# Where ScalarE's first "up" conversion stands in the experts' loop, and which engine makes the gate rows of the first layer

## Chip, cores and metric

The kernel runs on one core of one Trainium2 chip. The metric is the device time of one execution in microseconds (us). A profiled execution also leaves its span (first to last instruction) and, for each instruction, its start, its duration and what it waited for.

## The reference

The reference is two layers of a diffusion backbone over 512 latent and 256 context tokens of width 1024. Each layer has a token mixer (retention and pooling) and then a hierarchical mixture of 32 SwiGLU experts. Only the second half matters here:

```
h  = modulate(x, norm2_g, sh2, sc2)            # latent tokens, and in layer 0 the context tokens too
y  = sum over the token's 2 experts of  w * ((silu(h @ w_gate[e]) * (h @ w_up[e])) @ w_down[e])
x  = x + g2 * y        # latent rows use g2, context rows use cg2
```

`w_gate` and `w_up` of an expert are 1024 x 512, `w_down` is 512 x 1024, all float32: 2 MB each, 6 MB an expert, 32 experts a layer. The first layer routes 768 tokens (latent and context), the second only the 512 latent ones. So in the first layer a row that comes out of an expert is multiplied by `g2` or by `cg2`, as its token is latent or context; in the second layer all rows use `g2`.

## The kernel before

**Slots.** Each expert works on 96 slots (`CAP`). For each expert GpSimd gathers the slots' rows of `h` by an indirect DMA (`fetch`, L1215), TensorE turns them (`turn`, L1227), and VectorE and ScalarE copy the result out of PSUM (`turned`, L1231: `xh` on VectorE at L1234, `xl` on ScalarE at L1235).

**Weights.** All weights stream from HBM as 1 MB halves into a pool of 7 buffers named `raw`, issued by SyncE in one fixed order: for each expert two halves of gate, two of down (of the expert before) and two of up. `pump` (L141) issues the next transfers when VectorE's low conversion has been queued. ScalarE makes the float16 high part (`hi_`, which calls `conv_hi`, L1337), VectorE the float16 rest (`lo_`, which calls `conv_lo`, L1342). The second half of down is used as it is (`native`). TensorE multiplies high and low parts in three passes (`mm3`, L418 to L420), and the native half in float32 (L1285).

**The loop.** `for e in range(1, NE)` (L1545) writes out by hand the order of work of one expert on every engine; each engine runs its own instructions in that order. TensorE's order in a turn of the loop is: gate product of expert e+1, down product of e in two halves (n = 0 and 1), the transposes for e+2, up product of e+1. ScalarE's order is: the two gate conversions of e+2, `act_gate`, the first down conversion of e+1, `down_out` of half 0, the first up conversion of e+2 (L1575), `down_out` of half 1, the copy `xl`, the second up conversion. `down_out` (L1289) moves a half of the down product out of PSUM, times the routing weight of the slot.

**The gate rows.** `rows_of(e)` (L1487) gives the 96 x 1024 rows of gate factors of the expert's slots. In the second layer (`nv == 1`) these are the plain `g2` rows. In the first (`nv == 2`) `gate_rows` (L1291) works them out on GpSimd in two operations (L1296, L1297), from a tile `g2r` that holds `g2` and the difference of `cg2` and `g2`, and a flag of each slot (`ctx`, 1 for a context token). GpSimd then multiplies the expert's rows by them (`scatter`, L1305), starts the scatter that adds the rows to the stream in HBM (L1309), and the next `fetch`. Two `ye` tiles hold the experts' rows in turn; the gate rows lie in the second half of the same tile.

**The last expert** leaves the loop early: it skips scatter, and `last_down` (L1439) and `add_last` (L1451) add it on chip to the rows that were loaded back from HBM.

Of the kernel before, what the change touches and what calls it, by code (L numbers as in the profile page):

```python
# [14 lines left out]
ALU = mybir.AluOpType  # L15
# [11 lines left out]
CAP = 96  # L27
# [14 lines left out]
def kernel(ctx: ExitStack, tc: tile.TileContext, a: dict, out: bass.AP):  # L42
# [10 lines left out]
    def G(shape, dt, name):  # L53
        return pg.tile(shape, dt, name=name, tag="G")
# [4 lines left out]
    def W(shape, dt, name="wt"):  # L59
        return pw.tile(shape, dt, name=name, tag="W")  # L60
# [4 lines left out]
    def P(shape, name="pt"):  # L65
        return pp.tile(shape, F32, name=name, tag="P")

    V, A, Q, T = nc.vector, nc.scalar, nc.gpsimd, nc.tensor
# [317 lines left out]
    def mod_rows(l, sec, nv=2, tmp_=True):  # L386
        t = (R if tmp_ else G)([128, nv, D], F32, "modrow")
        nc.scalar.dma_start(out=t, in_=modr[l][sec, 0:nv].unsqueeze(0).to_broadcast([128, nv, D]))
        return t
# [791 lines left out]
    def make_sel(dst, posb, tiles, eng=None):  # L1181

        for i in tiles:
            (eng or Q).tensor_scalar(dst[:, i, :], iot1, posb[:, i, :], None, op0=ALU.is_equal)
# [28 lines left out]
    def fetch(l, xg, si):  # L1213

        Q.indirect_dma_start(  # L1215
            out=xg, out_offset=None, in_=hs[l],
            in_offset=bass.IndirectOffsetOnAxis(ap=si, axis=0), bounds_check=(6 - 2 * l) * 128 - 1,
            oob_is_err=False)

    def turn(xg):  # L1220

        out = []
        for r in range(2):
            pt = pp.tile([128, KC, CAP], F16, name="pgx", tag="P")
            for c in range(KC):
                o = r * D + c * 128
                T.transpose(pt[:, c, :], xg[0:CAP, o:o + 128], ident16[0:CAP, 0:CAP])  # L1227
            out.append(pt)
        return out

    def turned(pts):  # L1231
        xh = W([128, KC, CAP], F16, "xh")
        xl = W([128, KC, CAP], F16, "xl")
        V.tensor_copy(xh, pts[0])  # L1234
        A.copy(xl, pts[1])  # L1235
        return xh, xl
# [16 lines left out]
    def gate_up(w, xe, out_ps):  # L1253
        hi, lo = w
        xh, xl = xe
        for f in range(4):
            sl = slice(f * 128, (f + 1) * 128)
            for c in range(KC):
                mm3(out_ps[:, f, :], hi[:, c, sl], lo[:, c, sl], xh[:, c, :], xl[:, c, :], c == 0, c == KC - 1)

    def act_gate(pg_):
        sg = W([128, 4, CAP], F32, "sg")
        A.activation(sg, pg_, AF.Silu, scale=IWS)
        return sg

    def act_mult(pu, sg):

        V.scalar_tensor_tensor(sg[:, 0:2], pu[:, 0:2], IWS, sg[:, 0:2], op0=ALU.mult, op1=ALU.mult)
        V.tensor_tensor(sg[:, 2:4], pu[:, 2:4], sg[:, 2:4], op=ALU.mult)

    def act_split(sg):
        at = W([128, 2, 2, CAP], F16, "at")
        A.copy(at[:, 0], sg[:, 0:2])  # L1273
        V.tensor_tensor(at[:, 1], sg[:, 0:2], at[:, 0], op=ALU.subtract)
        return at

    def down_mm(w, raw, at, sg, n):

        hi, lo = w
        sl = slice(n * 512, (n + 1) * 512)  # L1280
        pt = P([128, 512], "pdn")
        for f in range(2):
            mm3(pt[0:CAP, :], at[:, 0, f, :], at[:, 1, f, :], hi[:, f, sl], lo[:, f, sl], f == 0, False)
        for f in range(2, 4):
            T.matmul(pt[0:CAP, :], lhsT=sg[:, f, :], rhs=raw[:, f - 2, sl], start=False, stop=(f == 3))  # L1285
        return pt

    def down_out(pt, wcol, yt, n):
        A.activation(yt[0:CAP, n * 512:(n + 1) * 512], pt[0:CAP, :], AF.Copy, scale=wcol)  # L1289

    def gate_rows(yg, ctx, g2r, nv):  # L1291

        if nv == 1:
            return [g2r[0:CAP, 0, n * 512:(n + 1) * 512] for n in range(2)]
        gn = yg[0:CAP, 1, :]
        Q.tensor_scalar(gn, g2r[0:CAP, 1, :], ctx, None, op0=ALU.mult)  # L1296
        Q.tensor_tensor(gn, gn, g2r[0:CAP, 0, :], op=ALU.add)  # L1297
        return [gn[:, n * 512:(n + 1) * 512] for n in range(2)]

    def scatter(l, yg, si, gs, eng):  # L1300

        yt = yg[:, 0, :]
        for n in range(2):
            yn = yt[0:CAP, n * 512:(n + 1) * 512]
            eng.tensor_tensor(yn, yn, gs[n], op=ALU.mult)  # L1305
        scatter_rows(l, yg, si)
# [9 lines left out]
    def new_conv(l, e, m):  # L1316
        if m == 2:
            t = G([128, 2, 2, 1024], F16, "wd")
            convs[l, e, m] = (t[:, 0], t[:, 1])
            return  # L1320
        convs[l, e, m] = (G([128, KC, 512], F16, "whi"), G([128, KC, 512], F16, "wlo"))
# [10 lines left out]
    def conv_hi(l, e, m, hf):  # L1332
        k_ = 4 if m < 2 else 2
        sl = slice(k_ * hf, k_ * hf + k_)
        hi, lo = convs[l, e, m]
        t = get("exp", l, e, m, hf)
        A.activation(hi[:, sl, :], t, AF.Copy, scale=WS)  # L1337
        return lo[:, sl, :], t, hi[:, sl, :]

    def conv_lo(low):  # L1340
        lo, t, hi = low
        V.scalar_tensor_tensor(lo, t, WS, hi, op0=ALU.mult, op1=ALU.subtract)  # L1342
        pump()

    def moe(l, h2, rt, pe0, nt, post_load=None):
# [80 lines left out]
        def load_latent(eng=nc.sync):  # L1426
            for i in range(4):
                eng.dma_start(out=xl[i // 2][:, i % 2, :], in_=xs[l][i * 128:(i + 1) * 128, :])

        def sel_transposed(pe):  # L1430

            pt = P([128, 512], "pst")
            for i in range(4):
                T.matmul(pt[0:CAP, i * 128:(i + 1) * 128], lhsT=pe[:, i, :], rhs=ident16, start=True, stop=True)
            t = W([128, 512], F16, "selT")
            A.copy(t[0:CAP], pt[0:CAP])
            return t
# [28 lines left out]
        def hi_(e, m, hf):  # L1466
            if hf == 0:
                new_conv(l, e, m)
            lows.append(conv_hi(l, e, m, hf))

        def lo_():
            conv_lo(lows.pop(0))

        def native(e):
            natives[l, e] = get("exp", l, e, 2, 1)

        def weight(e):
            return rt.sv[0:CAP, 0, e:e + 1]

        def slot(e):  # L1480
            return rt.si[:, e:e + 1]
# [5 lines left out]
        def rows_of(e):  # L1487
            yg = yes[e % 2]
            return yg, gate_rows(yg, rt.sv[0:CAP, 1, e:e + 1], g2r, nv)
# [12 lines left out]
        g2r = mod_rows(l, 3, nv, False)  # L1502
# [42 lines left out]
        for e in range(1, NE):  # L1545

            nx, nx2 = e + 1 < NE, e + 2 < NE
            act_mult(put, sg)
            at = act_split(sg)
            if lows:  # L1550
                lo_()
            sgd = sg
            w, raw = convs.pop((l, e, 2)), natives.pop((l, e))
            yg, gs = rows_of(e)
            if e == NE - 2:
                st["depth"] = NR - 2
            if e == NE - 4:
                pes = W([128, nt, CAP], F16, "pe")
                make_sel(pes, posm[:, :, NE - 1:NE], range(4))
            if not nx:  # L1560
                break
            pgt = P([128, 4, CAP], "pgate")
            gate_up(convs.pop((l, e + 1, 0)), xe, pgt)
            if nx2:
                for hf in range(2):
                    hi_(e + 2, 0, hf)
                    lo_()
            sg = act_gate(pgt)
            hi_(e + 1, 2, 0)
            native(e + 1)  # L1570
            lo_()
            pt = down_mm(w, raw, at, sgd, 0)
            down_out(pt, weight(e), yg[:, 0, :], 0)
            if nx2:
                hi_(e + 2, 1, 0)  # L1575
            pt = down_mm(w, raw, at, sgd, 1)
            down_out(pt, weight(e), yg[:, 0, :], 1)
            scatter(l, yg, slot(e), gs, Q)
            if nx2:
                xn = turned(turn(xg[:, e % 2]))  # L1580
                lo_()
                hi_(e + 2, 1, 1)
                if e + 4 < NE:
                    fetch(l, xg[:, e % 2], slot(e + 4))
            else:
                xl += [G([128, 2, D], F32, "xl") for _ in range(2)]
                load_latent()
                selT = sel_transposed(pes)
                if post_load:
                    post_load()  # L1590
            put = P([128, 4, CAP], "pup")
            gate_up(convs.pop((l, e + 1, 1)), xe, put)
            xe = xn
            if e == 8:
                rt.overflow()
# [205 lines left out]
```

## Time and profile before

| what | value |
|---|---|
| median of 3 runs | 1801.63 us (1801.56 to 1804.43) |
| time of the profiled execution | 1806.32 us |
| its span | 1804.5 us |
| TensorE busy | 1607.9 us, 89% of the span |
| VectorE busy | 1360.3 us, 75% |
| ScalarE busy | 1019.1 us, 56% |
| GpSimd busy | 1040.6 us, 58% |
| DMA moved | 542.33 MB, 301 GB/s over the span |
| granted TensorE clock, mean | 0.943 of full speed |

The shares are means over stages of different kinds. The experts' loops run from about 388 to 970 us (first layer) and from about 1240 to 1787 us (second layer). The two loops are the same code over weights of the same size, except for the gate rows and the number of routed rows, so each can be read against the other.

### The profile page before, as it was taken

How to read it: one execution, taken by the hardware profiler on the slowest of the kernel's cores; microseconds unless marked ns; L12 is line 12 of the kernel's file. 1: busy time of each engine (PE TensorE's matmuls, PEld its weight loads, DVE VectorE, ACT ScalarE, POOL GpSimd, SP SyncE). 2: the span in 40 equal slices, each digit the busy share in tenths (PEclk: the TensorE clock that was granted, in tenths of full speed). 3: DMA queues.
4: the chain of work that ended last, by engine and by line, in shares of the span. 5: the costliest groups of instructions: out<-in, count | busy, mean ns of one | idle time of the engine just before them, and what ended most of it. 6: DMA issues, size and time to landing. Idle time of an engine off the chain costs nothing. (4 is left out here: it accounts for less than half of the span.)

```text
span 1804.5 us, 43422 instructions
## 1 busy us (share of the span) xinstructions
PE 1607.9 (89%) x19059; PEld 1175.6 (65%) x19059; DVE 1360.3 (75%) x1454; ACT 1019.1 (56%) x1040; POOL 1040.6 (58%) x530
## 2 busy tenths in 40 slices
PE   6999998869897898988888999987999898999986
PEld 3577775556765676766664667645777777777763
DVE  5665567788788999887777786777977777778774
ACT  4433342337666667666664544434867667777762
POOL 1222224546898899999986232253455556666653
PEclk9999999969998999899998999987999999999998
DMA  9644455459998999999997165657999999999993
GB/s 386 246 143 182 149 204 216 149 197 326 381 367 337 355 391 393 382 369 378 364 370 241 55 216 170 238 198 247 371 391 373 377 393 388 399 398 391 395 373 124
DMA packets 127294, 542.33 MB, mean 301 GB/s; under 512 B 21595, under 2 KB 22667, under 8 KB 91001
## 3 DMA queue, kind: packets, MB, share of 16 engines
q1 hardware_dynamic: 105384, 507.87, 73.2%
q0 software_dynamic: 18000, 20.56, 4.8%
q10 hardware_dynamic: 3712, 11.04, 1.6%
q8 instruction: 153, 2.51, 0.6%
q14 instruction: 45, 0.36, 0.1%
HBM read 538.72 MB, written 45.69 MB: 324 GB/s over the span
## 5 line engine op out<-in xcount | busy, mean ns | idle before, releaser
L1342 DVE SCALAR_TENSOR_TENSOR wlo<-raw,whi 128x2048 f16<-128x2048 f32 x248 | 609.9, 2493 | 158.7 <-ACT whi L1337 157.5
L1337 ACT ACTIVATE whi<-raw 128x2048 f16<-128x2048 f32 x248 | 472.4, 1910 | 264.4 <-DMA raw<-in_exp_w_up_dram 212.5
L420 PEld LDWEIGHTS <-wlo 128*128 128x128 f16 x4512 | 454.8, 101 | 129.2 <-issue 97.9
L418 PEld LDWEIGHTS <-whi 128*128 128x128 f16 x4512 | 455.6, 101 | 45.6 <-issue 16.3
L419 PEld LDWEIGHTS <-whi 128*128 128x128 f16 x4512 | 455.2, 101 | 44.3 <-issue 15.0
L419 PE MATMUL pgate<-xl,whi 128*128 128x96 f16 x2048 | 299.2, 217 | 88.9 <-ACT xl L1235 88.6
L418 PE MATMUL pgate<-xh,whi 128*128 128x96 f16 x2048 | 302.7, 217 | 7.7 <-DVE xh L1234 5.5
L420 PE MATMUL pgate<-xh,wlo 128*128 128x96 f16 x2048 | 299.3, 217 | 0.0
L1305 POOL TENSOR_TENSOR ye<-ye,modrow 96x512 f32<-96x512 f32 x62 | 160.9, 2595 | 212.0 <-ACT ye L1289 212.0
L418 PE MATMUL pup<-xh,whi 128*128 128x96 f16 x2048 | 266.3, 206 | 0.0
L420 PE MATMUL pup<-xh,wlo 128*128 128x96 f16 x2048 | 266.0, 206 | 0.0
L419 PE MATMUL pup<-xl,whi 128*128 128x96 f16 x2048 | 266.0, 206 | 0.0
L1285 PE MATMUL pdn<-raw,sg 128*96 128x512 f32 x512 | 247.2, 606 | 0.0
L1309 POOL DMA_INDIRECT xs<-ye,si x63 | 192.3, 3052 | 23.6 <-POOL ye L1305 17.7
L1342 DVE SCALAR_TENSOR_TENSOR wd<-raw,wd 128x2048 f16<-128x2048 f32 x64 | 161.7, 2526 | 12.3 <-ACT wd L1337 11.9
L1305 POOL TENSOR_TENSOR ye<-ye 96x512 f32<-96x512 f32 x62 | 133.8, 2171 | 41.8 <-ACT ye L1289 40.0
L1296 POOL TENSOR_SCALAR ye<-modrow,sv 96x1024 f32<-96x1024 f32 x32 | 148.0, 4626 | 1.3
L1285 PEld LDWEIGHTS pdn<-raw,sg 128*96 128x96 f32 x512 | 85.6, 167 | 90.7 <-issue 72.1
L1337 ACT ACTIVATE wd<-raw 128x2048 f16<-128x2048 f32 x64 | 122.1, 1908 | 13.3 <-DMA raw<-in_exp_w_down_dram 13.2
L418 PE MATMUL pdn<-wd,at 128*96 128x512 f16 x256 | 99.8, 390 | 17.7 <-ACT at L1273 10.2
L405 DVE SCALAR_TENSOR_TENSOR wlo<-raw,whi 128x2048 f16<-128x2048 f32 (+1 forms) x36 | 84.8, 2361 | 39.4 <-ACT whi L404 39.4
L1215 POOL DMA_INDIRECT xg<-hs,si x62 | 89.2, 1439 | 34.3 <-issue 15.6
(310 smaller groups left out, 3123.9 us busy)
## 6 DMA issues: line engine op xcount, KB each, us to landing
raw<-in_exp_w_gate_dram SPq DMA_DIRECT2D x128, 1024.0 KB
raw<-in_exp_w_up_dram SPq DMA_DIRECT2D x128, 1024.0 KB
raw<-in_exp_w_down_dram SPq DMA_DIRECT2D x128, 1024.0 KB
raw<-in_ada_w_dram SPq DMA_DIRECT2D x32, 1024.0 KB
raw<-in_w_in_dram SPq DMA_DIRECT2D x20, 1024.0 KB
raw<-in_ada_dram SPq DMA_DIRECT2D x16, 1024.0 KB
raw<-in_w_out_dram SPq DMA_DIRECT2D x8, 1024.0 KB
xs<-xr ACTq DMA_DIRECT2D x10, 512.0 KB
```

What stands on the lines that cost most here:

```text
L405: V.scalar_tensor_tensor(lo, t, WS, hi, op0=ALU.mult, op1=ALU.subtract)
L418: T.matmul(o, lhsT=lh, rhs=rh, start=first, stop=False)
L419: T.matmul(o, lhsT=lh, rhs=rl, start=False, stop=False)
L420: T.matmul(o, lhsT=ll, rhs=rh, start=False, stop=last)
L1215: Q.indirect_dma_start(out=xg, out_offset=None, in_=hs[l], in_offset=bass.IndirectOffsetOnAxis(ap=si, axis=0), bounds_check=(6 - 2 * l) * ...
L1285: T.matmul(pt[0:CAP, :], lhsT=sg[:, f, :], rhs=raw[:, f - 2, sl], start=False, stop=(f == 3))
L1296: Q.tensor_scalar(gn, g2r[0:CAP, 1, :], ctx, None, op0=ALU.mult)
L1305: eng.tensor_tensor(yn, yn, gs[n], op=ALU.mult)
L1309: Q.indirect_dma_start(out=xs[l], out_offset=bass.IndirectOffsetOnAxis(ap=si, axis=0), in_=yg[0:si.shape[0], 0, :], in_offset=None, bounds ...
L1337: A.activation(hi[:, sl, :], t, AF.Copy, scale=WS)
L1342: V.scalar_tensor_tensor(lo, t, WS, hi, op0=ALU.mult, op1=ALU.subtract)
```

## The change

Two edits. In the first layer the row of `g2` of the slots is made by one VectorE operation in place of two GpSimd ones. In the loop the first up conversion on ScalarE stands after the second `down_out` and the copy `xl`, no longer between the two `down_out`.

```diff
         gn = yg[0:CAP, 1, :]
-        Q.tensor_scalar(gn, g2r[0:CAP, 1, :], ctx, None, op0=ALU.mult)
-        Q.tensor_tensor(gn, gn, g2r[0:CAP, 0, :], op=ALU.add)
+        V.scalar_tensor_tensor(gn, g2r[0:CAP, 1, :], ctx, g2r[0:CAP, 0, :], op0=ALU.mult, op1=ALU.add)
         return [gn[:, n * 512:(n + 1) * 512] for n in range(2)]
...
             pt = down_mm(w, raw, at, sgd, 0)
             down_out(pt, weight(e), yg[:, 0, :], 0)
-            if nx2:
-                hi_(e + 2, 1, 0)
             pt = down_mm(w, raw, at, sgd, 1)
             down_out(pt, weight(e), yg[:, 0, :], 1)
             scatter(l, yg, slot(e), gs, Q)
             if nx2:
                 xn = turned(turn(xg[:, e % 2]))
+                hi_(e + 2, 1, 0)
                 lo_()
                 hi_(e + 2, 1, 1)
```

`Q` is GpSimd, `V` VectorE. `hi_(e + 2, 1, 0)` is the conversion of the first half of `w_up` of expert e+2. On VectorE the new operation stands where `rows_of(e)` is called (L1554): after `act_split` and the low conversion of the second up half, ahead of the low conversions of gate.

## Rows read from the trace of the kernel before

**Rows 1.** Timeline of GpSimd: scatter starts of experts 0, 2, 30, in both layers.
```profile
411.25 1.64 POOL L1309 DMA_INDIRECT xs<-ye,si  x1 [0.28 <-POOL ye L1305]
...
457.65 3.65 POOL L1309 DMA_INDIRECT xs<-ye,si  x1 [0.28 <-POOL ye L1305]
...
958.38 1.60 POOL L1309 DMA_INDIRECT xs<-ye,si  x1 [0.49 <-POOL ye L1305]
...
1261.85 1.62 POOL L1309 DMA_INDIRECT xs<-ye,si  x1 [0.29 <-POOL ye L1305]
...
1304.02 3.64 POOL L1309 DMA_INDIRECT xs<-ye,si  x1 [0.28 <-POOL ye L1305]
...
1773.38 1.57 POOL L1309 DMA_INDIRECT xs<-ye,si  x1 [0.28 <-POOL ye L1305]
```
**Rows 2.** Windows: busy us by engine, then granted clock, DMA share, GB/s.
```profile
458.00:940.00 482.00, 422.05 (x6020) 327.63 (x6017) 413.99 (x258) 315.68 (x265) 445.05 (x163) 0.95 0.98 370
580.00:660.00 80.00, 73.29 (x1120) 58.60 (x1119) 78.96 (x44) 52.85 (x47) 68.23 (x26) 0.96 0.97 368
1304.00:1757.00 453.00, 415.38 (x6127) 324.88 (x6125) 340.81 (x256) 317.23 (x266) 270.58 (x110) 0.97 1.01 389
1760.00:1763.00 3.00, 3.00 (x42) 3.00 (x40) 2.52 (x5) 1.16 (x2) 2.72 (x2) 0.52 0.28 116
```
**Rows 3.** DMA queues, 458 to 940 us: packets, MB, share of 16 engines.
```profile
q1 hardware_dynamic: 29937, 167.67, 88.9%
q0 software_dynamic: 7619, 10.02, 8.6%
```
**Rows 4.** DMA queues, 1304 to 1757 us.
```profile
q1 hardware_dynamic: 30136, 168.50, 93.5%
q0 software_dynamic: 7632, 6.87, 6.4%
```
**Rows 5.** DMA queues, 1440 to 1720 us.
```profile
q1 hardware_dynamic: 18895, 105.90, 95.0%
q0 software_dynamic: 4906, 3.74, 5.7%
```
**Rows 6.** GpSimd by line, 458 to 940 us: busy, mean ns, idle before.
```profile
L1296 POOL TENSOR_SCALAR ye<-modrow,sv 96x1024 f32<-96x1024 f32 x27 | 127.8, 4732 | 1.1
L1305 POOL TENSOR_TENSOR ye<-ye 96x512 f32<-96x512 f32 x52 | 113.6, 2198 | 18.2 <-ACT ye L1289 16.6
...
L1297 POOL TENSOR_TENSOR ye<-ye,modrow 96x1024 f32<-96x1024 f32 x27 | 75.7, 2803 | 2.3
```
**Rows 7.** VectorE by line, 458 to 940 us.
```profile
L1342 DVE SCALAR_TENSOR_TENSOR wlo<-raw,whi 128x2048 f16<-128x2048 f32 x107 | 288.6, 2734 | 50.7 <-ACT whi L1337 50.7
```
**Rows 8.** VectorE by line, 1304 to 1757 us.
```profile
L1342 DVE SCALAR_TENSOR_TENSOR wlo<-raw,whi 128x2048 f16<-128x2048 f32 x107 | 241.1, 2287 | 81.8 <-ACT whi L1337 81.7
```
**Rows 9.** Source line L328, whole span: ns min/median/max, first and last start.
```profile
L328 DVE SCALAR_TENSOR_TENSOR acc<-raw,sel,acc x56: 1273/1279/2222, 107.4 to 1157.0; 128x1024 f32<-128x1024 f32 x56
```
**Rows 10.** Waits, 1304 to 1757 us: total us, times, longest us.
```profile
PE pgate L419 <- ACT xl L1235: 37.6, 21, 3.8
```
**Rows 11.** Timeline near the end of layer two's loop: TensorE, ScalarE, VectorE.
```profile
1752.82 0.25 PE L1227 MATMUL pgx<-ident,xg 96*128 96x96 f16 x2
...
1755.93 1.91 ACT L1337 ACTIVATE whi<-raw 128x2048 f16<-128x2048 f32 x1 [3.37 <-DMA raw<-in_exp_w_up_dram]
1757.75 0.67 ACT L1289 ACTIVATE ye<-pdn,sv 96x512 f32<-96x512 f32 x1
1758.32 0.78 ACT L1235 COPY xl<-pgx 128x768 f16<-128x768 f16 x1
...
1759.15 0.20 PE L419 MATMUL pgate<-xl,whi 128*128 128x96 f16 x1 [1.96 <-ACT xl L1235]
...
1761.46 2.28 DVE L1342 SCALAR_TENSOR_TENSOR wlo<-raw,whi 128x2048 f16<-128x2048 f32 x1
...
1771.04 0.21 PE L418 MATMUL pup<-xh,whi 128*128 128x96 f16 x1
```

## The prediction

> **What bounds the kernel now.** I read the page first, then the experts' loop of each layer as a window, since only these stages change, and then queues, lines and waits inside them. GpSimd's scatter starts give the pace of an expert: from expert 2 to 30 the first layer takes 958.38 - 457.65 = 500.7 us, 17.88 us an expert, and the second 1773.38 - 1304.02 = 469.4 us, 16.76 us [rows 1]. The code and the weights are the same size, so 1.12 us an expert is what the first layer pays for gate rows and for more routed rows. The windows show 27 experts each (482 / 17.88 and 453 / 16.76).
>
> In the second layer the transfers set the pace: the DMA engines' share is 1.01, at 389 GB/s, and no compute engine is near its limit but TensorE, 415 of 453 us busy [rows 2]. By queue, weights (q1) and gathers and scatters (q0) take 93.5 + 6.4 = 99.9% [rows 4]; its quiet middle has 95.0 + 5.7 = 100.7% [rows 5]. The reader should see that more speed of an engine cannot shorten that middle. In the first layer the queues take 88.9 + 8.6 = 97.5% [rows 3]. Scatters weigh more there, and that stays; but 2 to 3% of the time the transfers are not all asked for. Two engines are the suspects. GpSimd is busy 445 of 482 us, VectorE 414 of 482, and 78.96 of 80 us in the stretch 580 to 660 [rows 2]. VectorE's low conversion frees the buffer for the next transfer, and it takes 2734 ns against 2287 ns in the second layer [rows 7, 8].
>
> A second loss is the order on ScalarE. The first up conversion waits for its transfer, and behind it, in order, stand `down_out` and the copy `xl`, for which TensorE waits before the next gate product: 37.6 us in 21 waits in the second layer [rows 10]. While transfers set the pace this wait costs nothing by itself; after the last transfer it does.
>
> **The change, part by part. Gate rows.** GpSimd loses (127.8 + 75.7) / 27 = 7.5 us an expert [rows 6] of 445 / 27 = 16.5 us [rows 2], and is left with 9.0 us, far from the pace. VectorE gains one operation of 96 x 1024 float32 with a scalar per partition. Nearest row: the same kind at 128 x 1024 takes 1279 ns by the median, 1273 to 2222 [rows 9]. I take 1.28 us; the upper end is 2.22 us. VectorE now has 414 / 27 = 15.3 us an expert against 340.8 / 27 = 12.6 in the second layer [rows 2]. The loop of the second layer has all of GpSimd's remaining work, so I take its 12.6 and add 1.28: 13.9 us. If no conversion gets faster it is 15.3 + 2.2 = 17.5, still under 17.88 but no longer in the stretch 580 to 660. The operation writes the half of `ye` that the multiplies of two experts ago read; these ended about an expert's time earlier, so no wait. Behind it on VectorE stand the two gate conversions, and behind those the issue of two transfers, which go out 1.28 us later with three or more 1 MB transfers still in the queue: hidden while that queue is filled, 1.28 x 27 = 35 us at most if it were not.
>
> *What it gives in the first layer's loop.* Lower bound 0, if the missing 2.5% is the scatters' own irregularity. If the queues reach the second layer's share, 482 x (1 - 97.5 / 99.9) = 11.6 us [rows 3, 4]; if they reach the share of its quiet middle, 482 x (1 - 97.5 / 100.7) = 15.3 us [rows 5]. I take 11.6, the row of the same loop with its same interruptions. At the loop's start, experts 0 to 2, the first layer takes 457.65 - 411.25 = 46.4 us and the second 42.2 [rows 1]: 0 to 4.2 us, I take 2.
>
> The low conversions are longer by 2734 - 2287 = 447 ns beside GpSimd's gate rows [rows 7, 8]. The Trainium skill ("SBUF — State Buffer", Who interferes with whom) says that a VectorE instruction with two SBUF inputs and a GpSimd instruction that reads SBUF exclude each other for the whole instruction. By that rule the new operation could itself stand behind a whole GpSimd multiply of 2.2 us (an estimate by that page and the multiply's row), which would put VectorE at about 12.6 + 1.28 + 2.2 = 16.1 us; still under the pace, so the sum stays. The trace agrees in kind: conversions are slowed, though not each by a whole GpSimd operation.
>
> **Order on ScalarE.** Nothing is added or removed; the conversion issues no transfer itself, and on ScalarE it is moved past a `down_out` of 0.67 us and a copy of 0.78. On the queue of VectorE its low conversion keeps its place. In the last expert but one of layer two, the transposes end at 1753.07, so both could end by about 1754.5, while the weights came at 1755.93 [rows 11]: 1.4 us of margin, so the conversion is not later. TensorE no longer waits. If the transposes ended after the weights' arrival, the conversion would be late by the difference, hidden by the queued transfers. So in the paced part of layer two I take 1 us, of 0 to 453 x (1 - 99.9 / 100.7) = 3.6 us that its queues leave unused [rows 4, 5].
>
> *At the ends.* After the last up weights, TensorE's work is what is left. In layer two it waits 1.96 us for `xl` until 1759.15, and its granted clock over the next 3 us is 0.52 [rows 2, 11], nearly the 1.2 GHz level of its two (1.2 and 2.4 GHz), after that idle: 3 x 0.48, about 1.5 us more. So at least 3.5 us. TensorE's lead may also build up, by 37.6 / 27 = 1.4 us an expert, until the next thing it needs, the low part of the second up half: that ends at 1761.46 + 2.28 = 1763.7, and the up product starts at 1771.04 [rows 11]. So at most 7.3 us; I take 5, half-way. The first layer's end has the same code, then the overflow check and conversions for the next layer, which may swallow it: 0 to 7.3, I take 3.
>
> **Sum.** 11.6 + 2 + 1 + 5 + 3 = 22.6 us. The profiled execution takes 1806.3 us, 1.8 over its span; 1806.3 - 22.6 = 1783.7. It lies 4.7 us over the median of the runs, so against 1801.6 the forecast is 1779.0. A difference under 0.2%, 3.6 us, is about what cannot be told from none.
>
> **Rivals.**
> *Transfers at their limit already.* The first layer's loop keeps its 500 us since its scatters (8.6% against 6.4% of the engines [rows 3, 4]) use what seems unused; only ends gain. For it: a share of 0.98 in the window [rows 2]. Against: 370 GB/s there, 389 in the second loop. Time: 1801.6 - 5 - 2 = 1794.6. A page speaks for it: the Trainium skill ("SBUF — State Buffer", A bandwidth-pool intuition that's wrong) gives about 358 GB/s from HBM to a core, by which both loops are above the limit and nothing is left to gain. The trace differs, with 389 GB/s over 453 us [rows 2].
> *VectorE becomes the bound.* Conversions stay at 2734 ns because the multiplies, not the gate rows, slow them, and the new operation takes 2.2 us. Place: 580 to 660, where VectorE is 99% busy; 4.5 experts x 2.2 = 10 us there, and no lead for TensorE in layer one. Time: 1801.6 + 10 - 5 = 1806.6, slower. It decides if VectorE's time an expert passes the transfers' pace. Against: 12.6 us in layer two beside the same multiplies.
> *The change does nothing.* TensorE's wait for `xl` is replaced by one for weights just as late, also at the ends, and GpSimd's work was off the path: 1801.
>
> **How the numbers follow.** Forecast 0.66, transfers at their limit 0.20, nothing 0.08, VectorE the bound 0.06. All lower terms together give 3.5 us, all upper ones 15.3 + 4.2 + 3.6 + 7.3 + 7.3 = 37.7 us, hence 1764 to 1798; leaving out the corners and the two last rivals, the range is 1767 to 1797. Faster 0.86, same 0.08, slower 0.06.
>
> **What would show it.** In the profile after: GpSimd's lines of gate rows gone and 32 VectorE operations of about 1.3 us; low conversions of the first layer near 2.29 us; an expert of the first layer near 17.4 us and one of the second near 16.7; queue shares in the first loop near 100%; no wait of the gate product for `xl`; the up product of the last expert of layer two nearer to its low conversion. The prediction is wrong if the queue shares stay at 97.5% while VectorE and GpSimd have fallen, if VectorE's new operation takes over 2 us, or if ScalarE stands idle before the moved conversion with its weights already there.

## The result, and the profile after

The changed kernel takes 1779.6 us by the median (1778.7 to 1781.3 in 4 runs) against 1801.6 us, in the ratio 0.988 with an interval of 0.986 to 0.990: about 22 us faster, at 1.2% some six times what can be told from no change. Run again beside another 13 runs of the kernel before it gave 0.989 (0.986 to 0.992). The forecast was 1779.0 us. The total came out; half of the terms did not, and most of what follows is about them. The profiled execution took 1778.7 us, 0.9 under its own median, where that of before lay 4.7 over its own; so the two traces differ by 27.6 us, and some 5.6 of these are not the change's. To keep them out I took a second profile of the kernel before (label `e13_before_again`, 1796.0 us), and below a difference is shown against both.

Windows of the profile after, 27 experts of each layer as in [rows 2], then the two stretches in which experts 8 to 12 of the first layer and the former bottleneck lie. Columns: busy us of TensorE, weight load, VectorE, ScalarE, GpSimd, then granted clock, DMA share, GB/s.

```profile
444.00:926.00 482.00, 422.95 (x6169) 320.88 (x6168) 381.20 (x292) 326.43 (x272) 242.43 (x112) 0.98 1.00 379
1277.00:1730.00 453.00, 413.20 (x6098) 315.01 (x6096) 341.18 (x258) 323.14 (x269) 216.02 (x110) 0.98 1.01 389
533.14:600.89 67.75, 61.52 (x915) 47.18 (x916) 61.56 (x61) 47.90 (x41) 45.05 (x16) 0.97 0.99 380
580.00:660.00 80.00, 76.22 (x1159) 58.82 (x1157) 70.11 (x50) 57.86 (x49) 48.54 (x22) 1.00 1.02 402
```

GpSimd has 242 / 27 = 9.0 us an expert instead of 16.5, VectorE 381 / 27 = 14.1 instead of 15.3, with an operation more. In 580 to 660, where it was 79 of 80 us busy [rows 2], VectorE now has 10 us free. The second layer's row moves little. The granted clock of the first loop is 0.98 and was 0.95 [rows 2]; TensorE has some 60 us of the 482 idle in both, and no run separates the clock from the rest. The queues of the first window, to be read beside [rows 3]:

```profile
q1 hardware_dynamic: 31220, 171.21, 90.3%
q0 software_dynamic: 7858, 10.47, 9.0%
```

Together 99.3% and not 97.5%. VectorE by line in the same window, beside [rows 7] (busy us, mean ns, idle before):

```profile
L1341 DVE SCALAR_TENSOR_TENSOR wlo<-raw,whi 128x2048 f16<-128x2048 f32 x109 | 252.3, 2330 | 69.2 <-ACT whi L1336 69.2
L1296 DVE SCALAR_TENSOR_TENSOR ye<-modrow,sv 96x1024 f32<-96x1024 f32 x28 | 35.7, 1274 | 0.0
L1274 DVE TENSOR_TENSOR at<-sg,at 128x192 f16<-128x192 f32 x27 | 9.9, 367 | 7.0 <-ACT at L1273 7.0
...
L1268 DVE SCALAR_TENSOR_TENSOR sg<-pup,sg 128x192 f32<-128x192 f32 x27 | 9.4, 348 | 0.0
```

The low conversion fell from 2734 to 2330 ns, and the gate row costs 1274 ns. A row that I had not read ahead of the prediction fell further: the small subtraction that makes the low part of `at` took 1004 ns in the first trace of before, and takes 367. GpSimd by line shows what is left there, beside [rows 6]:

```profile
L1304 POOL TENSOR_TENSOR ye<-ye 96x512 f32<-96x512 f32 x54 | 115.2, 2150 | 217.0 <-ACT ye L1289 216.9
```

Waits of TensorE in the same window (total us, times, longest us). The wait for `xl` [rows 10] is gone, here and in the second layer. Another has taken its place: the down product waits for the cast `at`, which stands on ScalarE behind the second up conversion.

```profile
PE pdn L418 <- ACT at L1273: 38.1, 24, 4.1
...
PE pgate L418 <- DVE xh L1234: 20.7, 17, 2.8
```

The scatter starts of experts 2 and 30, the anchors of [rows 1], in both layers:

```profile
444.13 3.37 POOL L1308 DMA_INDIRECT xs<-ye,si  x1 [0.28 <-POOL ye L1304]
...
932.42 1.55 POOL L1308 DMA_INDIRECT xs<-ye,si  x1 [0.28 <-POOL ye L1304]
...
1275.13 3.36 POOL L1308 DMA_INDIRECT xs<-ye,si  x1 [0.28 <-POOL ye L1304]
...
1744.69 1.55 POOL L1308 DMA_INDIRECT xs<-ye,si  x1 [0.28 <-POOL ye L1304]
```

An expert of the first layer takes (932.42 - 444.13) / 28 = 17.44 us (17.88 before), one of the second 16.77 (16.76). These anchors mislead a little, since the second `down_out` no longer stands behind a conversion and so the scatter itself comes earlier. From here on an expert is timed by VectorE's first multiply of the up product (line 1268). The table has the us between these multiplies, one profile a row.

| kernel | L1 0→2 | 2→8 | 8→12 | 12→31 | L2 2→30 | 30→31 |
|---|---|---|---|---|---|---|
| before, first profile | 54.9 | 106.0 | 78.9 | 333.6 | 472.8 | 15.2 |
| before, second profile | 55.1 | 104.1 | 77.3 | 332.0 | 473.8 | 13.6 |
| order only (e1) | 55.6 | 106.9 | 70.5 | 339.6 | 473.0 | 11.4 |
| gate row only (e2) | 48.9 | 106.5 | 70.0 | 332.7 | 474.4 | 13.6 |
| order, gate row for 0 to 2 (e11) | 48.1 | 107.8 | 77.4 | 345.0 | 472.8 | 11.4 |
| order, gate row for 7 to 14 (e12) | 54.9 | 107.9 | 66.6 | 339.4 | 472.9 | 11.4 |
| after plus a VectorE operation (e9) | 50.5 | 105.7 | 72.6 | 337.4 | 473.0 | 11.4 |
| after | 46.9 | 107.0 | 67.8 | 333.5 | 472.6 | 11.4 |
| after, again (e6) | 47.8 | 106.7 | 68.0 | 331.8 | 473.3 | 11.4 |

Between before and after the reader should see three places and nothing else: the start of the first loop, 55 to 47 us; experts 8 to 12 of it, 77 to 79 down to 68; and the last step of the second loop, 13.6 or 15.2 to 11.4. The paced parts (2→8, 12→31, 2→30) do not move between before and after. Each row is one execution: those of e1, e11 and e12 stood 8 us under, 10 over and 7 over the median of their kernels; so the columns say where, and the medians how much.

In e1, e11 and e12, which have the new order and gate rows on GpSimd for most experts, 12→31 is long. So the loss behind expert 8 is not tied to the column 8→12. Two other sums show it in every row. The step 8→9 takes 23.8 to 26.2 us in the four profiles with the gate row of expert 9 on GpSimd (before twice, e1, e11), and 20.8 to 21.9 in the other five (in the second loop, without gate rows, 20.7 to 22.3). And 8→31 takes 412.5 and 409.3 us in before, 410.1 with the order alone, 422.5 in e11, against 401.2 and 399.9 after.

### The profile page after: what moved, and what is told of

Its sections match the earlier page's. It is cut to its first block, busy times and chain, and to the rows that moved or that the text cites. A ratio compares the mean times of both kernels' runs of the same rounds, so it can differ in the third digit from the quotient of the medians.

```text
span 1776.9 us, 43385 instructions
## 1 busy us (share of the span) xinstructions
PE 1591.1 (90%) x19059; PEld 1146.2 (65%) x19059; DVE 1315.5 (74%) x1486; ACT 1028.0 (58%) x1040; POOL 752.6 (42%) x466
## 5 line engine op out<-in xcount | busy, mean ns | idle before, releaser
L1341 DVE SCALAR_TENSOR_TENSOR wlo<-raw,whi 128x2048 f16<-128x2048 f32 x248 | 568.8, 2315 | 158.9 <-ACT whi L1336 158.6
L419 PEld LDWEIGHTS <-whi 128*128 128x128 f16 x4512 | 442.8, 98 | 71.1 <-issue 41.8
L418 PEld LDWEIGHTS <-whi 128*128 128x128 f16 x4512 | 443.3, 98 | 45.6 <-issue 16.3
L420 PEld LDWEIGHTS <-wlo 128*128 128x128 f16 x4512 | 442.7, 98 | 36.2 <-issue 5.0
L418 PE MATMUL pgate<-xh,whi 128*128 128x96 f16 x2048 | 269.8, 207 | 31.6 <-DVE xh L1234 31.0
L419 PE MATMUL pgate<-xl,whi 128*128 128x96 f16 x2048 | 269.7, 207 | 0.4 <-ACT xl L1210 0.2
L420 PE MATMUL pgate<-xh,wlo 128*128 128x96 f16 x2048 | 269.7, 207 | 0.0
L1304 POOL TENSOR_TENSOR ye<-ye,modrow 96x512 f32<-96x512 f32 x62 | 124.2, 2018 | 260.0 <-ACT ye L1289 260.0
L1336 ACT ACTIVATE wd<-raw 128x2048 f16<-128x2048 f32 x64 | 122.2, 1910 | 78.9 <-DMA raw<-in_exp_w_down_dram 78.9
L1308 POOL DMA_INDIRECT xs<-ye,si x63 | 135.6, 2152 | 21.3 <-POOL ye L1304 17.7
L1215 POOL DMA_INDIRECT xg<-hs,si x62 | 121.7, 1962 | 32.2 <-issue 24.2
L418 PEld LDWEIGHTS <-at 128*96 128x96 f16 x256 | 32.4, 127 | 113.0 <-ACT at L1273 78.4
```

The source lines that it names most:

```text
L418: T.matmul(o, lhsT=lh, rhs=rh, start=first, stop=False)
L419: T.matmul(o, lhsT=lh, rhs=rl, start=False, stop=False)
L420: T.matmul(o, lhsT=ll, rhs=rh, start=False, stop=last)
L1215: Q.indirect_dma_start(out=xg, out_offset=None, in_=hs[l], in_offset=bass.IndirectOffsetOnAxis(ap=si, axis=0), bounds_check=(6 - 2 * l) * ...
L1308: Q.indirect_dma_start(out=xs[l], out_offset=bass.IndirectOffsetOnAxis(ap=si, axis=0), in_=yg[0:si.shape[0], 0, :], in_offset=None, bounds ...
```

## Experiments

My theory after the result: gate rows on GpSimd cost time only through VectorE, whose operations they slow, in two places where VectorE has no slack; the transfers set the rest. Rivals: GpSimd's own time was the bound (late scatters and gathers); the gain is spread over all experts; the order on ScalarE gives the larger part.

**Each part alone.** `e1_order_only` puts the gate row of the changed kernel back on GpSimd:

```
-        V.scalar_tensor_tensor(gn, g2r[0:CAP, 1, :], ctx, g2r[0:CAP, 0, :], op0=ALU.mult, op1=ALU.add)
+        Q.tensor_scalar(gn, g2r[0:CAP, 1, :], ctx, None, op0=ALU.mult)
+        Q.tensor_tensor(gn, gn, g2r[0:CAP, 0, :], op=ALU.add)
```

> The moved conversion alone; the gate rows stay on GpSimd in two operations. The prediction's terms for the order are 1 us in the paced part of layer two and 5 + 3 us at the two ends: 1801.6 - 9 = 1792.6 us, no wait of the gate product for xl, and GpSimd and VectorE of the first loop as busy as before. Rival 'the gate rows carry it all': 1800 to 1802 us. Rival 'the order carries it, since the wait for xl was on the path of every expert': below 1785 us.

`e2_gate_only` puts the changed kernel's first up conversion back between the two `down_out`:

```
             down_out(pt, weight(e), yg[:, 0, :], 0)
+            if nx2:
+                hi_(e + 2, 1, 0)
             pt = down_mm(w, raw, at, sgd, 1)
...
                 xn = turned(turn(xg[:, e % 2]))
-                hi_(e + 2, 1, 0)
```

> The gate rows on VectorE alone; the first up conversion stays between the two copies of the down product. The prediction's terms are 11.6 us in the first layer's loop and 2 us at its start: 1801.6 - 13.6 = 1788.0 us, the second layer as before. Rival 'the gate rows carry it all': 1779 to 1781 us. Rival 'the order carries it': 1797 to 1801 us.

Order alone: 1807.6 us, ratio 1.001 (0.999 to 1.003), no gain, where its terms in the forecast came to 9 us. Gate row alone: 1786.7 us, ratio 0.990 (0.987 to 0.993), 18 us of the 22. Waits of TensorE in the first layer's window (444 to 926 us) with the order alone:

```profile
PE pdn L418 <- ACT at L1273: 39.0, 15, 11.0
```

In before the same engine waited for `xl` in that window:

```profile
PE pgate L419 <- ACT xl L1235: 42.2, 19, 4.4
```

One wait was exchanged for another of the same size, on the same engine, behind the other half of the same conversion. That is the rival "the change does nothing", for this part.

**Where the gate row's gain lies.** In `e11_first_three` the gate row is on VectorE for experts 0 to 2 alone, in `e12_middle_eight` for 7 to 14 alone; the others keep GpSimd's two operations, and both have the new order. A flag handed to `gate_rows` chooses the form; each kernel has one of the two added lines.

```
-            return yg, gate_rows(yg, rt.sv[0:CAP, 1, e:e + 1], g2r, nv)
+            return yg, gate_rows(yg, rt.sv[0:CAP, 1, e:e + 1], g2r, nv, e < 3)        # e11
+            return yg, gate_rows(yg, rt.sv[0:CAP, 1, e:e + 1], g2r, nv, 6 < e < 15)   # e12
```

> The new order, and the gate row on VectorE for experts 0, 1 and 2 alone; the others have the two GpSimd operations. If 8 us of the gain come from the start of the loop (experts 0 to 2 take 47 us and not 55) and the rest from experts 8 to 12, the start is short here, the stretch 8 to 12 is as in before, and the time is 6 to 9 us under before, ratio 0.995 to 0.9965. If the gain is spread evenly over the 32 experts, 3 of 32 give some 2 us, ratio 0.999.

> The new order, and the gate row on VectorE for experts 7 to 14 alone, around the counting of the overflow, where VectorE was 99% busy; the others have the two GpSimd operations. If 10 us come from that stretch, experts 8 to 12 take about 68 us, the start stays at 55, and the time is 7 to 11 us under before, ratio 0.994 to 0.996. If the gain is spread evenly, 8 of 32 give some 5 us, ratio 0.997. If the stretch's long time in the first profile of before was of that one run, nothing is gained, ratio 1.000.

> The kernel before once more, for a second profile. If the two places found in its first profile belong to the kernel, experts 0 to 2 of the first layer take 54 to 56 us, experts 8 to 12 take 77 to 80, and the step from expert 30 to 31 of the second layer about 15; if the long stretch from 8 to 12 was of that one run, it takes about 70 here, as in the kernel with the new order alone, and the loop's gain has to be looked for elsewhere. The ratio is 1.000.

Three experts give 1795.9 us, ratio 0.995 (0.993 to 0.997); eight give 1788.8 us, ratio 0.992 (0.990 to 0.995); before once more gives 1.000 (0.998 to 1.002), and its second profile has the same two long places as its first (its last step of the second loop, 13.6 us, is shorter than the 15 expected). The shares, 0.5% and 0.8%, add up to 1.2%, all that the change gives, though both hold the order's share too; evenly spread they would have been 3 and 8 of 32 parts, 2 and 5 us. So the gain is not spread: e11 has only the start short, e12 only 8→12. The 14 us of e12 are more than the 7 to 11 expected, and more than 8→12 alone lost in either trace of before. Windows of the second profile of before: experts 8 to 12, then a part of it.

```profile
539.61:616.88 77.27, 64.94 (x968) 49.82 (x966) 71.43 (x57) 48.22 (x41) 68.17 (x27) 0.97 0.92 341
560.00:600.00 40.00, 31.55 (x450) 23.34 (x448) 39.02 (x37) 23.79 (x22) 35.17 (x15) 0.96 0.86 315
```

And experts 8 to 12 of `e12_middle_eight`:

```profile
546.76:613.32 66.56, 60.28 (x886) 45.95 (x887) 60.82 (x61) 47.78 (x41) 42.44 (x15) 0.97 0.99 377
```

In before the transfers fall to 0.86 in those 40 us while VectorE is 39 us busy; with the gate row moved they run at 0.99 through the stretch. What happens at 558 us, in VectorE's timeline of that second profile (start, us, line, operation, idle before):

```profile
558.44 1.03 DVE L1167 TENSOR_SCALAR ov<-ov 128x32 f32<-128x32 f32 x1
559.51 2.33 DVE L1170 SCALAR_TENSOR_TENSOR ov<-ov 128x32 f32<-128x32 f32 x6
...
564.20 1.15 DVE L1274 TENSOR_TENSOR at<-sg,at 128x192 f16<-128x192 f32 x1 [0.21 <-ACT at L1273]
565.28 9.91 DVE L1342 SCALAR_TENSOR_TENSOR wlo<-raw,whi 128x2048 f16<-128x2048 f32 x3
```

The counting of the overflow, a one-off behind expert 8, occupies VectorE from 558.2 to 563.5 us, and the three low conversions behind it take 3.3 us each. Each of them frees a weight buffer, so the transfers fall back. The counting takes 5.2 us here, 7.3 in the first profile of before and 8.6 in e1 and e11; it takes 3.4 in the trace after (550.56 to 553.99) and in e12.

Behind it VectorE has to catch up. Between experts 10 and 12 it is 99% busy in both profiles of before (95 and 91% in those after), and from 12 to 16 still 97 and 99% (84 and 83%). How long this lasts differs: in the profile of e11 VectorE is 98% busy from expert 9 to 22, at 17.9 us an expert, with the transfers at 0.96:

```profile
566.07:798.69 232.62, 203.67 (x2898) 157.35 (x2899) 228.67 (x119) 154.44 (x130) 202.99 (x76) 0.95 0.96 358
```

So the loss begins at the counting in each profile with GpSimd's gate rows there; where it ends, and with it the time of one execution, varies.

**Is it VectorE's time or GpSimd's?** `e9_vector_one_more` adds one VectorE operation an expert, on rows that nobody reads; `e4_vector_more` adds two. `e3_gpsimd_writes` and `e5_gpsimd_writes_5` add eight and five GpSimd memsets there, which write only. Each kernel has one of the two loops below.

```
         V.scalar_tensor_tensor(gn, g2r[0:CAP, 1, :], ctx, g2r[0:CAP, 0, :], op0=ALU.mult, op1=ALU.add)
+        for _ in range(1):   # e9; 2 in e4
+            V.scalar_tensor_tensor(yg[CAP:128, 1], g2r[CAP:128, 1, :], 1.0, g2r[CAP:128, 0, :], op0=ALU.mult, op1=ALU.add)
+        for _ in range(8):   # e3; 5 in e5
+            Q.memset(yg[CAP:128, 1], 0.0)
```

> The changed kernel with one more VectorE operation an expert in the first layer (the same kind as the gate row, on the 32 partitions that nobody reads, about 1.22 us), so that VectorE has about 15.3 us an expert again, as it had before the change, while GpSimd keeps its 12 us. If before lost its time because VectorE had no slack (its low conversions made longer beside GpSimd's gate rows), this kernel loses most of what the loop gained: experts 8 to 12 of the first layer take 74 to 79 us and not 68, and the time is 8 to 12 us over that of the changed kernel, ratio to before 0.993 to 0.995. If GpSimd's own time was what before lost to, this kernel stays within 3 us of the changed one, ratio 0.988 to 0.990.

> The changed kernel, and in the first layer two more VectorE operations of 1.28 us an expert with the same operands, into 32 unused partitions: VectorE has 2.6 us more, about 16.7 us an expert against 15.3 in the kernel before, with GpSimd as in the changed one. If VectorE's time set the pace in the first loop, nearly all of its 12 us gain is lost: 1790 us or more, with the stretch after expert 8 the worst. If VectorE's time is covered by the transfers, 1779 to 1783 us.

> The changed kernel, and in the first layer GpSimd also clears 32 x 1024 elements eight times an expert, some 7.5 us, where the two operations of the gate rows stood; nothing of it is read. It gives GpSimd its time back without reading SBUF. If the gate rows on GpSimd cost time by slowing VectorE's conversions, the time stays near the changed kernel's, 1779 to 1783 us, with conversions near 2.3 us. If they cost time because GpSimd was full and its multiplies, scatters and gathers came late, the 13.6 us of the gate rows come back: about 1793 us.

> As the clearing experiment, with five clears instead of eight, some 5 us: what the two gate-row operations take on GpSimd when nothing stands in their way (2.87 + 2.33 us). GpSimd is then busy about 14 us an expert and has slack. If what cost time was GpSimd without any slack, so that gathers and the last scatter came late, the time goes back to within 5 us of the changed kernel's and TensorE's waits for gathered rows vanish. If any time on GpSimd costs, it lies half-way, 12 us or more above the changed kernel.

One more operation: 1789.5 us, ratio 0.993 (0.990 to 0.995), some 8 us lost by the ratios, with GpSimd at half load. Two: 1813.6 us, ratio 1.005 (1.003 to 1.007), some 30 us lost. The first layer's window of the two, `e9_vector_one_more` and then `e4_vector_more`:

```profile
444.00:926.00 482.00, 420.49 (x6203) 326.46 (x6201) 437.09 (x317) 321.54 (x268) 256.08 (x110) 0.98 0.99 374
```

```profile
444.00:926.00 482.00, 409.10 (x5893) 321.19 (x5890) 473.64 (x331) 306.71 (x257) 297.64 (x107) 0.95 0.96 358
```

With one more, VectorE is 437 of 482 us busy, 16.2 us an expert; before had 15.3. Only 1.2 of the 2.1 us more than after are the added operation; the rest is conversions that got longer, those for the down product from 2288 to 2942 ns. Over the window the transfers are near 0.99, but from expert 9 to 19 VectorE is 98% busy, at 17.3 us an expert:

```profile
558.31:731.26 172.95, 151.55 (x2233) 116.61 (x2234) 170.25 (x112) 118.56 (x100) 101.83 (x40) 0.98 0.97 374
```

The kernel loses in 0→2 (3 us), 8→12 (nearly 5) and 12→31 (4 to 6): 8→31 takes 410.0 us, as in before. At 474 us VectorE is the bound of the whole loop. The time lost was as expected. The stretch 8→12 was not (72.6 us where 74 to 79 were), nor VectorE's load (16.2 us an expert where 15.3 were); and GpSimd had 9.5 us an expert, not the 12 that the expectation says. So with GpSimd half idle VectorE's time alone, at a load somewhat above that of before, brings back all that before lost behind expert 8. In all it brings back a good third: at the start, where before had operations made longer on the chain that TensorE waits for, it loses only 3 of 8 us.

The memsets cost as much, but not in the same way. Five: 1793.5 us, ratio 0.994 (0.993 to 0.996), 12 us above the changed kernel, as the second case of the expectation has it; eight: 1810.8 us, ratio 1.003 (1.002 to 1.005), some 27 us, which is more than either case. The low conversions stay at 2383 and 2310 ns, and TensorE waits for something that it never waited for in before, the gathered rows. VectorE's low conversions and TensorE's wait in `e3_gpsimd_writes`, first layer's window:

```profile
L1343 DVE SCALAR_TENSOR_TENSOR wlo<-raw,whi 128x2048 f16<-128x2048 f32 x108 | 247.9, 2310 | 55.5 <-ACT whi L1338 52.6 <-issue 2.7
```

```profile
PE pgx L1227 <- DMA xg<-hs,si: 34.8, 14, 3.9
```

GpSimd at its limit would thus cost time too, but through late gathers, and no such wait stands in either trace of before. In `e5_gpsimd_writes_5` I had left GpSimd an idle reserve on paper; it was 445 of 482 us busy all the same, because its other operations stretched: the multiplies to 2875 ns (2150 after), the gathers to 3131 ns (2070).

Two things blur these two runs. In `e3_gpsimd_writes` 11 us of the loss lie behind the loop: from its last multiply to the first of layer two it takes 295.2 us, 282 to 285 in all other profiles, since the last expert's eight memsets stand there on GpSimd (956.3 to 964.3 us) and TensorE waits 10.5 us for that expert's rows. And memsets left the conversions alone, but not VectorE's small copies: the counting takes 6.2 us in both kernels, four of its copies some 0.97 us each where they take 0.17 after.

**Further order.** `e7_at_ahead` moves the second up conversion behind the cast `at` of the next expert, to take the new wait away too:

```
             if lows:
                 lo_()
+            if e > 1 and nx:
+                hi_(e + 1, 1, 1)
+                lo_()
...
                 hi_(e + 2, 1, 0)
-                lo_()
-                hi_(e + 2, 1, 1)
```

> The changed kernel, with the second up conversion moved behind the cast and split of the activations (at) of the next turn of the loop, and the low part of the first up half behind them too: the down product no longer waits for a cast that stands behind the arrival of the second up half (29 us in layer two, 38 us in layer one). If transfers set the pace of both loops, only TensorE's lead at the ends can gain: 0 to 5 us below the changed kernel. If TensorE's wait is on the path of every expert, 20 us or more below it.

> The changed kernel once more, beside the kernel before on the chip of the runs that follow: a ratio near 0.988. Against the gate rows alone (ratio 0.990) this says what the order adds: 0 to 0.3%.

1781.1 us, ratio 0.988 (0.985 to 0.991), the same as the changed kernel on that chip (1781.5). TensorE's wait moved once more, in the first layer's window:

```profile
PE pgate L418 <- DVE xh L1234: 54.3, 23, 4.1
```

**Do transfers set the pace?** `e8_less_bytes` transfers only half of the second half of each `w_down`, the native one, so half a MB of 6 an expert is left out, and multiplies twice with the row block that it has; its output is another one.

```
-            nc.sync.dma_start(out=t, in_=src)
+            if key[0] == "exp" and key[3:] == (2, 1):
+                nc.sync.dma_start(out=t[:, 0:1], in_=src[:, 0:1])
+            else:
+                nc.sync.dma_start(out=t, in_=src)
...
-            T.matmul(pt[0:CAP, :], lhsT=sg[:, f, :], rhs=raw[:, f - 2, sl], start=False, stop=(f == 3))
+            T.matmul(pt[0:CAP, :], lhsT=sg[:, f, :], rhs=raw[:, 0, sl], start=False, stop=(f == 3))
```

> The changed kernel, in which half of each expert's native half of w_down is not transferred and the other half stands in for it in the product (so the output is another): 5.5 MB an expert instead of 6, all instructions of the engines as before. If transfers set the pace of both loops, each expert gets shorter by about 7.5%, up to TensorE's 15.7 us an expert: some 40 to 70 us in all. If an engine sets it, less than 10 us.

1717.9 us, ratio 0.953 (0.949 to 0.956), 64 us under the changed kernel on the same chip, with no engine's work reduced. From expert 2 to 31 the first loop goes from 508.2 to 479.4 us, the second from 484.0 to 451.9: 5.7% and 6.6% for 8% of the weights' bytes. The window of its first loop:

```profile
444.00:905.00 461.00, 425.52 (x6262) 324.46 (x6259) 414.97 (x293) 328.10 (x275) 360.60 (x116) 0.98 0.99 369
```

## Why the prediction was right in total, and where it was not

**The bound.** Right for the second loop and for most of the first. `e8_less_bytes` shows that the transfers pace both loops after the change, and 2→30 of the second does not move with any order on ScalarE. In the first loop of before VectorE set the pace for a while behind the counting, 99% busy between experts 10 and 12 with the transfers at 0.95.

**Cost of the new operation.** Right: 1274 ns (taken 1.28 us), VectorE 14.1 us an expert (13.9), GpSimd 9.0 (9.0), low conversions 2330 ns (near 2290). The reason was right as well: GpSimd's gate rows slowed VectorE's operations with two inputs in SBUF. VectorE by line in the second profile of before, first layer's window, shows which:

```profile
L1342 DVE SCALAR_TENSOR_TENSOR wlo<-raw,whi 128x2048 f16<-128x2048 f32 x108 | 297.9, 2795 | 47.5 <-ACT whi L1337 47.4
...
L1274 DVE TENSOR_TENSOR at<-sg,at 128x192 f16<-128x192 f32 x27 | 26.4, 979 | 14.2 <-ACT at L1273 14.2
...
L1268 DVE SCALAR_TENSOR_TENSOR sg<-pup,sg 128x192 f32<-128x192 f32 x27 | 9.3, 346 | 0.0
```

The subtraction `at` reads two SBUF tiles and takes 979 ns, 367 after; the multiply `sg` of the same shape has one input in PSUM and takes 346, and 348 after. The memsets, which read nothing, leave the conversions at 2310 ns. The Trainium skill ("SBUF — State Buffer", Who interferes with whom) has this distinction: two SBUF inputs on VectorE against a GpSimd instruction that reads SBUF, and not against one that only writes. All three rows agree with it. The distinction by two inputs does not cover everything that was slowed: the cast `rwt` below has one input and took 0.89 us in before and 0.26 after, and an operation of the counting with one input (line 1167) took 1.03 and 2.12 us in before and 0.18 after.

**First loop, 11.6 us.** The size was nearly right: experts 2 to 31 took 518.5 and 513.4 us in the two profiles of before and 508.2 and 506.6 in those after, 5 to 12 less. The place was wrong. I spread the missing 2.4% of the queues over the loop; between before and after it stood in one stretch, 8→12, whose shortening of 9 to 11 us is the whole term. What made it was a one-off, the counting, and VectorE's catching up behind it. I had the stretch before me, 79 of 80 us busy [rows 2], and used it for a rival only. That rival, VectorE becoming the bound, was a true limit and not far: `e9_vector_one_more` loses some 8 us with 2.1 us more of VectorE's time an expert.

**Start of the first loop, 2 us of 0 to 4.2.** Mis-sized: it gave 8. The bound came from the time between scatters 0 and 2, and scatter 0 itself is late for the same reason; part of the loss lies ahead of the window that I compared. VectorE's timeline there, in the second profile of before:

```profile
388.32 0.89 DVE L1146 CAST rwt<-rtmp 128x192 f16<-128x192 f32 x1
389.25 2.48 DVE L1148 TENSOR_TENSOR rtmp<-rtmp,rwt 128x192 f32<-128x192 f32 x1
...
413.95 2.96 DVE L1342 SCALAR_TENSOR_TENSOR wd<-raw,wd 128x2048 f16<-128x2048 f32 x1 [0.16 <-ACT wd L1337]
416.84 4.43 DVE L1342 SCALAR_TENSOR_TENSOR wlo<-raw,whi 128x2048 f16<-128x2048 f32 x1
```

and the same four in the trace after:

```profile
386.47 0.26 DVE L1146 CAST rwt<-rtmp 128x192 f16<-128x192 f32 x1
386.77 0.36 DVE L1148 TENSOR_TENSOR rtmp<-rtmp,rwt 128x192 f32<-128x192 f32 x1
...
408.00 2.29 DVE L1341 SCALAR_TENSOR_TENSOR wd<-raw,wd 128x2048 f16<-128x2048 f32 x1 [0.21 <-ACT wd L1336]
410.21 2.29 DVE L1341 SCALAR_TENSOR_TENSOR wlo<-raw,whi 128x2048 f16<-128x2048 f32 x1
```

The chain that makes the slots' values, on which TensorE waits, took 13.1 us beside the gate row of expert 0 and takes 9.6; two conversions beside that of expert 1 took 7.4 us and take 4.6. Together 6.3 us.

From expert 0 to 1 before took 40.2 and 40.8 us and after 33.1, 7 to 8 less. The rest lies between the two places, where VectorE waits for ScalarE, and ScalarE for the down product of expert 0: 7.4 and 8.0 us in before and 5.5 after. There 1.2 us are the new operation, which runs in this idle time and so costs nothing. The other 0.7 and 1.3 us are TensorE. Its down product takes 7.8 and 8.5 us in before and 7.1 after. Ahead of it TensorE waited 12.5 us for the chain in both profiles of before, 9.0 after, and it begins at the lower of the two clock levels, 1.2 GHz (granted 0.50, 0.50 and 0.53 in its first 2 us); in the next 2 us 0.67 and 0.50 are granted in before, and 1.00, which is 2.4 GHz, after. Its first 4 us in the first profile of before, then in the trace after (the granted clock is the last number but two):

```profile
401.05:405.05 4.00, 4.00 (x12) 1.90 (x10) 2.94 (x4) 0.80 (x1) 0.00 (x0) 0.58 0.07 8
```

```profile
391.94:395.94 4.00, 4.00 (x14) 1.84 (x12) 3.96 (x5) 0.80 (x1) 0.00 (x0) 0.76 0.00 0
```

So 3.5 + 2.8 + 0.7 us make 7.0 of the 7.1 by which the first profile of before is longer.

**Paced part of layer two, 1 us.** It gave nothing: 2→30 takes 472.6 us (472.8 and 473.8 before).

**End of layer two, 5 us of 3.5 to 7.3.** Mis-sized: 2.2 to 3.8 us, the last column of the table, 11.4 us in every row with the new order and in none without. TensorE did gain its lead, but I had named the wrong next limit, the low part of the second up half. In ScalarE's timeline after, the cast `at` stands behind the whole second up conversion, which waits for its transfer:

```profile
1731.07 1.91 ACT L1336 ACTIVATE whi<-raw 128x2048 f16<-128x2048 f32 x1 [1.28 <-DMA raw<-in_exp_w_up_dram]
1733.57 1.91 ACT L1336 ACTIVATE whi<-raw 128x2048 f16<-128x2048 f32 x1 [0.59 <-DMA raw<-in_exp_w_up_dram]
1735.66 0.35 ACT L1273 CAST at<-sg 128x192 f16<-128x192 f32 x1 [0.18 <-DVE sg L1268]
```

Whether this part shows in the time is open: the order alone gave 1.001, the order beside the gate row 0.988 against 0.990, with intervals that overlap.

**End of layer one, 3 us.** It gave nothing: from its last multiply to the first of layer two 283.7 us, 284.4 and 282.9 before.

**The sum.** Forecast 11.6 + 2 + 1 + 5 + 3 = 22.6 us; shown about 10 + 8 + 0 + 3 + 0 = 21, with the first term by 8→12 (by 2→31 it is 5 to 12). Gate rows were 13.6 of the forecast and are 18 of the gain, the order 9 and is at most 4. The total was right by luck: the start was taken 6 us too small, the order's terms some 6 us too large, and the two errors cancelled. Transfers at their limit already: fell, the share rose to 1.00 once VectorE kept up, and 379 to 389 GB/s stood over whole loops. No change: fell for the gate rows, held for the order within what can be measured.

## What to carry to other kernels

A share of 97% over a long window may be 100% nearly everywhere and 86% in one place, so cut the window until the loss stands alone, and look there for a one-off piece of work on an engine that has little slack, and for how long that engine then needs to catch up. When an engine's operation is slowed by a neighbour, list every operation that runs beside the neighbour's, the small ones on the critical chain too, and not the largest group alone. Moving an instruction behind a wait helps only if the next thing in the queue is not just as late; look for what TensorE needs next, one instruction further, on the same queue.

## Not expected of the hardware

GpSimd's busy time says little of its reserve. Its gathers (line 1215) of the same shape took 1438 ns in the mean in the second profile of before, 2070 after, 3131 in `e5_gpsimd_writes_5` and 6074 with the gate row alone, and in that last kernel nothing was late for it. What makes a gather longer is not shown: `e11_first_three`, with most gate rows on GpSimd, has 2114 ns, and the changed kernel once more 1749. Their row with the gate row alone, first layer's window:

```profile
L1215 POOL DMA_INDIRECT xg<-hs,si x26 | 157.9, 6074 | 7.9 <-issue 7.6 <-PE pgate L420 0.3
```

The runs also came closer together: 1777.5 to 1784.9 us in 12 runs of the changed kernel and of `e7_at_ahead`, against 1796.0 to 1813.3 for the kernel before. The order alone, with gate rows on GpSimd, spreads as wide, 1794.3 to 1812.5 us. That would fit VectorE's catching up behind the counting, which ended near expert 16 in both profiles of before and after 22 in that of e11; with one or two profiles a kernel it is only argued.
